# Stick-breaking attention: the queries' 1/rms inside the sigmoids, one scan for two heads, one split for two heads' result

## The chip, the core and the metric

The kernel runs on one core of a Trainium2 chip. That core has a tensor engine (PE, with its weight loads PEld), a vector engine (DVE), a scalar engine (ACT), a general engine (POOL), and a queue that issues loads (SP). Each of them works through its own list of instructions in order and waits on semaphores for the others. The metric is the device time of one execution in microseconds (us); lower is better.

## What is computed

A decoder trunk on 256 tokens of width 1024: one gMLP layer and one attention layer, each between two half-step SwiGLU FFNs, RMSNorm ahead of every part. The change is in the attention alone:

```python
def rms_norm(x, g):
    return x * lax.rsqrt(jnp.mean(x * x, axis=-1, keepdims=True) + NORM_EPS) * g

def one_block(qb, bi):                       # qb: (q * 1/sqrt(64)) of 128 queries, 16 heads
    mask = key_pos[None, :] < q_pos[:, None]
    z = jnp.einsum('bqkgd,bskd->bkgqs', qb, kf)
    log_1m_beta = jnp.where(mask, jax.nn.log_sigmoid(-z), 0.0)
    rev = lax.cumsum(log_1m_beta, axis=4, reverse=True)
    excl = jnp.concatenate([rev[..., 1:], jnp.zeros_like(rev[..., :1])], axis=-1)
    a = jnp.where(mask, jnp.exp(jax.nn.log_sigmoid(z) + excl), 0.0)
    return jnp.einsum('bkgqs,bskd->bqkgd', a, vf)

x = x + stick_breaking_attention(rms_norm(x, mix_norm) @ w_q, k, v) @ w_o
```

The kernel does this with products instead of sums of logarithms: a weight is sigmoid(z) times the product of sigmoid(-z) over the keys that lie between.

## The kernel before

**Products.** The residual stream lies transposed in SBUF (`xT`, features on partitions, tokens along the free axis). Every float32 operand is split into a high and a low part, and `mm3` (L145 to L150) makes each product of three matmuls: L148 high times low, L149 low times high, L150 high times high. `split` (L152 to L154) makes the parts: a cast on ACT, a subtraction on DVE. The weights stream in as 333 pieces of 128x1024, each loaded once and split by ACT (L81, `whi`) and DVE (L83, `wlo`) some pieces ahead of use. These splits run through the whole kernel, the attention too.

**1/rms.** `Rms.columns` (L305) makes 1/rms as two columns `rT`, one value per token on the partitions, and two diagonal blocks `diag` (L320). `Rms.rows` (L323) turns them into `rb`, the same values along the free axis on all partitions, with one product on PE (L324) and a copy on ACT (L325).

**Attention.** It goes by blocks of two heads, b = 0 to 7, in the order that `ATT_STEPS` writes down. For each block:
- q (`q_in`, `q_out`; one for four heads): 48 matmuls into a PSUM bank; L680 multiplies by 1/rms and 1/8 (`rb8`) on DVE into `qf`; then `qf` is split into `qh`, `ql`.
- z (`weights_of`): the scores of 128 queries at a time, so two banks per block: `z0` with 2x128 keys, `z1` with 2x256. ACT makes `keep` = sigmoid(-z) (L711) and `beta` = sigmoid(z) (L712). POOL masks both on the diagonal block (L718), and sets the last column of `keep` (L710).
- p (`products_of`): DVE runs the reversed product over `keep` with one scan per head and block of queries (L728), four per block of two heads; POOL (128 keys) or DVE (256 keys) multiplies it into `beta` (L729).
- t (`transposed`): six transposes on PE (L736 to L738) into two banks `at`, then splits into `a0h`, `a0l`, `a1h`, `a1l`.
- v (`values_of`): the products with v into a bank `o`; its two halves (one head each, on 64 partitions) are split into `oTh`, `oTl`, one after the other.
- o: 24 matmuls of `oT` with w_o into the four banks `yo`.

**What sets the order.** The program is traced in the order of `ATT_STEPS`, and a scheduler then orders each engine's list by priority and by its own model of durations, and puts in the waits. So an instruction that becomes shorter or goes away also moves others. Two limits matter here: the scores, transposes and results share four PSUM banks (pool `pg`), so a new z needs a bank that somebody has finished reading; and `beta`, `keep` and other short-lived tiles share eight SBUF buffers (pool `scr`).

Of the kernel before, what the change touches and what calls it, by code (L numbers as in the profile page):

```python
# [15 lines left out]
P = 128  # L16
T = 256
# [12 lines left out]
# The attention's order of issue, by blocks of two heads: q (four heads' queries), z (scores), p  # L30
# (weights), t (weights transposed), v (values), o (products into the residual stream, in the
# banks that y sets up).
# [6 lines left out]
class Weights:  # L39
    """The weight matrices as a stream of [128, 1024] pieces in the order of use. Each is loaded  # L40
    once and split exactly into two float32r parts, w = hi + lo, some pieces ahead of its use."""

    def __init__(self, tc, raw_pool, hi_pool, lo_pool):
# [3 lines left out]
        self.behind = 0  # so many pieces keep their place  # L47
# [12 lines left out]
    def order(self, ins):  # L60
        """Keeps an instruction behind those traced ahead of it, where the order matters."""
        return self.keep_order(ins) if self.strict else ins
# [37 lines left out]
def trunk(  # L100
# [44 lines left out]
    def mm3(o, a, b, first, last):  # L145
        """o (+)= a.T @ b for a, b each given as two float32r parts."""
# [9 lines left out]
    # The gMLP's blocks of 256 features: the u products, the mixing behind them, the products into  # L156
    # the residual stream behind that.
# [16 lines left out]
    def plan_in_out(n, ins, w_out):  # L174
        """Pairs of blocks: columns of the first matrix, then, one pair later, the rows that they
        meet in the second."""
# [66 lines left out]
    def warm_up(n):  # L243
        """Products of nothing, that wake the tensor engine's clock while the first loads run."""
        bank = gbank("warm")
        for _ in range(n):
            W.order(nc.tensor.matmul(bank[:, :P], ones, ones, start=True, stop=True))
# [17 lines left out]
    rb = act.tile([P, T], F32, name="rb")  # L265
    rT = act.tile([P, 2], F32, name="rT")
    diag = act.tile([P, 2, P], F32, name="diag")

    def prepare(d, gains, sq=True):
        """The parts of x*g of chunk d for the next products, and its share of the mean square."""  # L270
# [22 lines left out]
    def newton(o, root, v, w):  # L293
        """o = v**-0.5 from an estimate of v**0.5, with a step of Newton's; w is scratch."""
# [5 lines left out]
    class Rms:  # L300
        """1/rms of each token: first as a column per 128 tokens (rT), then along the free axis on
        all partitions (rb)."""
# [4 lines left out]
        def columns(self):  # L307
# [11 lines left out]
            for tt in range(2):  # L319
                nc.vector.tensor_scalar_mul(diag[:, tt, :], ident, rT[:, tt : tt + 1])  # L320
# [8 lines left out]
    def load_x(hf):  # L329
        """Half of x into the residual stream, its parts and its squares."""  # L330
# [33 lines left out]
    def bc2(ap):  # L364
        """[128, n] -> [128, 2, n], the same twice."""
# [6 lines left out]
    class Residual:  # L372
        """y.T = sum over chunks of W[chunk].T @ h[chunk], in four banks."""
# [13 lines left out]
    def close(y, tail, head, scale, gains):  # L387
        """The last chunks block by block, so that each block of x is ready early; head blocks of
        the first of them go ahead."""
# [11 lines left out]
    def project(outs, ids, xs, mid={}, by_bank=False):  # L401
        """outs += W.T x for blocks of 256 features: [features, tokens] of two halves each. mid:
        what else is done behind a number of groups."""
# [20 lines left out]
    def project_rows(o, ids, xs, mid={}):  # L424
        """x.T W for a block of 256 features: [tokens, features] of two halves."""
# [17 lines left out]
    def ffn_in(tag, j, ids, mid={}, by_bank=False):  # L443
        """silu(gate) * up of 256 features, in two parts."""
# [16 lines left out]
    def ffn(tag, plan, gains, mid={}, by_bank=False, extra={}):  # L461
        """extra: what else is done ahead of a block's products into the residual stream."""
# [439 lines left out]
```

## Time and profile before

| what | value |
|---|---|
| time, median of 3 runs | 1019.38 us (1019.08 to 1020.25) |
| span of the profiled execution, first to last instruction | 1016.9 us |
| PE busy in the span | 998.7 us (98%) |
| DVE, ACT, POOL busy | 651.4, 499.6, 84.0 us |
| the attention in the span, first q product to the last product with w_o | about 739 to 826 us |

The profile is of one execution, and its own total time isn't recorded beside the span; the median of the timed runs lies 2.4 us above the span, and what is saved inside the span is taken off the median. In the rows below, L numbers are lines of the kernel before. An idle time in brackets stands ahead of its instruction, with the instruction that ended the wait. A matmul's busy time overlaps the next one's: those of 256 columns are shown as 0.28 us and start 0.12 us apart.

### The profile page before, as it was taken

How to read it: one execution, taken by the hardware profiler on the slowest of the kernel's cores; microseconds unless marked ns; L12 is line 12 of the kernel's file. 1: busy time of each engine (PE TensorE's matmuls, PEld its weight loads, DVE VectorE, ACT ScalarE, POOL GpSimd, SP SyncE). 2: the span in 40 equal slices, each digit the busy share in tenths (PEclk: the TensorE clock that was granted, in tenths of full speed). 3: DMA queues.
4: the chain of work that ended last, by engine and by line, in shares of the span. 5: the costliest groups of instructions: out<-in, count | busy, mean ns of one | idle time of the engine just before them, and what ended most of it. 6: DMA issues, size and time to landing. Idle time of an engine off the chain costs nothing.

```text
span 1016.9 us, 19320 instructions
## 1 busy us (share of the span) xinstructions
PE 998.7 (98%) x8044; PEld 979.4 (96%) x8044; DVE 651.4 (64%) x852; ACT 499.6 (49%) x683; POOL 84.0 (8%) x122
## 2 busy tenths in 40 slices
PE   9999999999999999999999999999998899999997
PEld 8999999999999999999999999999998799999996
DVE  6865665676766774646569655564679975655553
ACT  7543434475544553434348444443476565444433
POOL 3000000010000300000003000000036420000002
PEclk9999999999999999999999999999999999999999
DMA  9965555656545365655564756555642436656511
GB/s 310 325 187 174 185 179 176 187 161 212 186 167 167 125 214 183 187 184 187 180 190 141 239 185 187 182 188 181 193 132 65 137 117 219 188 185 191 183 42 42
DMA packets 135208, 179.56 MB, mean 177 GB/s; under 512 B 5624, under 2 KB 119376, under 8 KB 135120
## 3 DMA queue, kind: packets, MB, share of 16 engines
q1 hardware_dynamic: 134768, 177.76, 54.9%
q8 instruction: 63, 1.03, 0.4%
q0 software_dynamic: 192, 0.52, 0.2%
q14 instruction: 25, 0.20, 0.1%
q10 hardware_dynamic: 160, 0.05, 0.0%
HBM read 176.73 MB, written 1.05 MB: 175 GB/s over the span
## 4 chain that ended last, share of the span: by engine, by line
PE 88%; DVE 6%; issue 2%; ACT 1%; DMA 1%; POOL 1%; SPq 0%; ACTq 0%; POOLq 0%; DVEq 0%
PE yo L148 2%; PE yo L150 2%; PE yo L149 2%; PE gb L148 2%; PE uc L149 2%; PE gc L148 2%; PE ub L149 2%; PE yb L148 2%; PE uc L150 2%; PE ub L150 2%; PE ub L148 2%; PE gb L150 2%; PE uc L148 2%; PE ud L150 2%; PE gc L150 2%
## 5 line engine op out<-in xcount | busy, mean ns | idle before, releaser
L81 ACT CAST whi<-raw 128x1024 fp32r<-128x1024 f32 (+1 forms) x333 | 342.3, 1044 | 403.3 <-issue 219.2
L83 DVE TENSOR_TENSOR wlo<-raw,whi 128x1024 fp32r<-128x1024 f32 (+1 forms) x333 | 400.9, 1221 | 203.2 <-ACT whi L81 202.4
L288 POOL TENSOR_TENSOR acc<-acc,sq 128x256 f32<-128x256 f32 x39 | 33.9, 870 | 566.9 <-ACT sq L287 564.9
L148 PE MATMUL ga<-xnh,wlo 128*128 128x256 f32 x176 | 50.7, 288 | 0.0
L148 PE MATMUL ya<-hha,wlo 128*128 128x256 f32 x176 | 50.0, 284 | 0.1
L148 PE MATMUL yc<-hhc,wlo 128*128 128x256 f32 x176 | 50.0, 284 | 0.1
L148 PE MATMUL yb<-hhb,wlo 128*128 128x256 f32 x176 | 50.0, 284 | 0.0
L148 PE MATMUL gd<-xnh,wlo 128*128 128x256 f32 x176 | 50.0, 284 | 0.0
L148 PE MATMUL gb<-xnh,wlo 128*128 128x256 f32 x176 | 49.9, 283 | 0.0
L148 PE MATMUL gc<-xnh,wlo 128*128 128x256 f32 x176 | 49.9, 283 | 0.0
L149 PE MATMUL ya<-hla,whi 128*128 128x256 f32 x176 | 49.8, 283 | 0.0
L149 PE MATMUL yb<-hlb,whi 128*128 128x256 f32 x176 | 49.8, 283 | 0.0
L149 PE MATMUL yc<-hlc,whi 128*128 128x256 f32 x176 | 49.7, 283 | 0.0
L150 PE MATMUL ud<-xnh,whi 128*128 128x256 f32 x176 | 49.7, 282 | 0.0
L150 PE MATMUL uc<-xnh,whi 128*128 128x256 f32 x176 | 49.6, 282 | 0.0
L149 PE MATMUL ub<-xnl,whi 128*128 128x256 f32 x176 | 49.6, 282 | 0.0
L149 PE MATMUL uc<-xnl,whi 128*128 128x256 f32 x176 | 49.6, 282 | 0.0
L150 PE MATMUL yb<-hhb,whi 128*128 128x256 f32 x176 | 49.6, 283 | 0.0
L148 PE MATMUL ua<-xnh,wlo 128*128 128x256 f32 x176 | 49.6, 282 | 0.0
L150 PE MATMUL ga<-xnh,whi 128*128 128x256 f32 x176 | 49.6, 282 | 0.0
L150 PE MATMUL ub<-xnh,whi 128*128 128x256 f32 x176 | 49.6, 282 | 0.0
L149 PE MATMUL gd<-xnl,whi 128*128 128x256 f32 x176 | 49.5, 281 | 0.0
(286 smaller groups left out, 3367.1 us busy)
## 6 DMA issues: line engine op xcount, KB each, us to landing
raw<-in_ffn_w_in_dram SPq DMA_DIRECT2D x176, 512.0 KB, 4.6
raw<-in_ffn_w_out_dram SPq DMA_DIRECT2D x88, 512.0 KB, 4.2
raw<-in_a_w_in_dram SPq DMA_DIRECT2D x32, 512.0 KB, 4.4
raw<-in_a_w_out_dram SPq DMA_DIRECT2D x16, 512.0 KB, 3.3
raw<-in_b_w_q_dram SPq DMA_DIRECT2D x8, 512.0 KB, 4.4
raw<-in_b_w_o_dram SPq DMA_DIRECT2D x8, 512.0 KB, 4.3
raw<-in_w_kv_dram SPq DMA_DIRECT2D x4, 512.0 KB, 4.2
xin<-in_x_dram SPq DMA_DIRECT2D x4, 256.0 KB, 4.5
```

The lines of the kernel that those rows point to most:

```text
L81: ins = nc.scalar.copy(hi[:, cc], raw[:, cc])
L83: ins = nc.vector.tensor_sub(lo[:, cc], raw[:, cc], hi[:, cc].bitcast(F32))
L148: nc.tensor.matmul(o, al, bh, start=first, stop=False, skip_group_check=True)
L149: nc.tensor.matmul(o, ah, bl, start=False, stop=False, skip_group_check=True)
L150: nc.tensor.matmul(o, ah, bh, start=False, stop=last, skip_group_check=True)
L288: nc.gpsimd.tensor_add(acc, acc, s)
```

## The change

Three edits in the attention, and one piece of memory that they need.

1. q isn't scaled any more: `q_out` splits the PSUM bank itself, without `qf`. The factor 1/rms/8 goes into the sigmoids as a scale per partition, since the scores have queries on partitions (`zscale`, two tiny tiles made from `rT`). So for this norm there is no `diag`, no product on PE and no `rb`.
2. One scan runs over both heads of a block of queries. `keep` of the two heads is one row of 2x(S+1) elements; the extra column of each head is 0 and not 1, and the scan's second operation adds a row that is 1 at the start of each head and 0 elsewhere, which restarts the product. That row is in `spare`, where `rb` and `diag` lie for the rest of the kernel; POOL fills it with four memsets.
3. The bank `o` is copied on ACT, 64 partitions at a time, into one tile `of`, and `of` is split by one cast and one subtraction over 128 partitions.

```diff
-    rb = act.tile([P, T], F32, name="rb")
     rT = act.tile([P, 2], F32, name="rT")
-    diag = act.tile([P, 2, P], F32, name="diag")
+    spare = act.tile([P, P + 1 + 2 * (T + 1)], F32, name="spare")
+    rb = spare[:, :T]
+    diag = spare[:, T : 2 * T].rearrange("p (n t) -> p n t", n=2)
...
             for tt in range(2):
-                nc.vector.tensor_scalar_mul(diag[:, tt, :], ident, rT[:, tt : tt + 1])
+                if self.tag != "m1":
+                    nc.vector.tensor_scalar_mul(diag[:, tt, :], ident, rT[:, tt : tt + 1])
...
     def q_out(j, bank):
-        qf = scratch(f"qf{j}")
-        nc.vector.tensor_mul(pair(qf), pair(bank), bc2(rb8))
...
-        split(qh, ql, qf)
+        split(qh, ql, bank)
...
-            nc.gpsimd.memset(keep[:, :, S : S + 1], 1.0)
-            nc.scalar.activation(keep[:, :, :S], z, AF.Sigmoid, scale=-1.0)
-            nc.scalar.activation(beta, z, AF.Sigmoid)
+            nc.gpsimd.memset(keep[:, :, S : S + 1], 0.0)
+            nc.scalar.activation(keep[:, :, :S], z, AF.Sigmoid, scale=zscale[1][:, tt : tt + 1])
+            nc.scalar.activation(beta, z, AF.Sigmoid, scale=zscale[0][:, tt : tt + 1])
...
-            for h in range(2):
-                rev = keep[:, h, :S][:, ::-1]
-                nc.vector.tensor_tensor_scan(rev, rev, rev, 1.0, ALU.mult, ALU.bypass)
+            rev = keep.rearrange("p h s -> p (h s)")[:, ::-1]
+            r0 = 0 if tt == 0 else P + 1
+            nc.vector.tensor_tensor_scan(
+                rev, rev, spare[:, r0 : r0 + 2 * (S + 1)], 0.0, ALU.mult, ALU.add
+            )
...
+        of = scratch(f"of{b}", T)
         for r in range(2):
             rr = slice(r * 64, (r + 1) * 64)
-            split(oT[0][rr, b, :], oT[1][rr, b, :], bank[rr, r * T : (r + 1) * T])
+            nc.scalar.copy(of[rr, :], bank[rr, r * T : (r + 1) * T])
+        split(oT[0][:, b, :], oT[1][:, b, :], of)
...
-    project([first[1]], [[i] for i in plan_q[1]], XN, {1: norm.rows})
-    nc.vector.tensor_scalar_mul(rb8, rb, 0.125)
+    project([first[1]], [[i] for i in plan_q[1]], XN)
+    for t, s in zip(zscale, (0.125, -0.125)):
+        nc.vector.tensor_scalar_mul(t, rT, s)
...
+    nc.gpsimd.memset(spare, 0.0)
+    for c in (0, P + 1, P + 1 + T + 1):
+        nc.gpsimd.memset(spare[:, c : c + 1], 1.0)
```

The lists of the engines change from the first q products on. On PE, around the transposes of block 0 (`at_0_...`), before; `q_9105` is q for heads 12 to 15, `z_0_8945` and `z_1_8954` are the scores of block 1:

```order
L150 MATMUL z_0_8945<-kzh,qh_8836 128x256
L148 MATMUL z_1_8954<-kzh,ql_8837 128x512
L149 MATMUL z_1_8954<-kzl,qh_8836 128x512
L150 MATMUL z_1_8954<-kzh,qh_8836 128x512
L148 MATMUL q_9105<-xnh,wlo_8731 128x256
L149 MATMUL q_9105<-xnl,whi_8730 128x256
L736 MATMUL at_0_8971<-ident,beta_0_8850 128x128
L150 MATMUL q_9105<-xnh,whi_8730 128x256
```

and after, the same place (`q_8873` is q for heads 8 to 11, `z_0_8980` the scores of block 2):

```order
L150 MATMUL q_8873<-xnh,whi_8700 128x256
L148 MATMUL z_0_8938<-kzh,ql_8832 128x256
L149 MATMUL z_0_8938<-kzl,qh_8831 128x256
L150 MATMUL z_0_8938<-kzh,qh_8831 128x256
L148 MATMUL z_1_8947<-kzh,ql_8832 128x512
L149 MATMUL z_1_8947<-kzl,qh_8831 128x512
L150 MATMUL z_1_8947<-kzh,qh_8831 128x512
L740 MATMUL at_0_8964<-ident,beta_0_8847 128x128
L741 MATMUL at_0_8964<-ident,beta_1_8856 128x128
L742 MATMUL at_0_8965<-ident,beta_1_8856 128x128
```

Before, the scores of block 0 stood behind 37 of the 48 products of the q for heads 8 to 11, and the first transpose of block 0 came 25 rows behind those scores, alone, with the other five after 14 more q products. After, the scores of block 0 stand ahead of all 48, the first transpose comes 60 rows behind them, and all six stand together. 24 products of the last q now stand together behind the transposes of block 2.

On DVE, the rows for block 6 before (`keep` is the scans):

```order
L728 SCALAR_TENSOR_TENSOR keep_0_9338<-keep_0_9338 128x128 x2
L728 SCALAR_TENSOR_TENSOR keep_1_9347<-keep_1_9347 128x256
L154 TENSOR_TENSOR oTl<-o_9359,oTh 64x256
L728 SCALAR_TENSOR_TENSOR keep_1_9347<-keep_1_9347 128x256
L154 TENSOR_TENSOR a0l_9385<-at_4_9376,a0h_9384 128x512
L154 TENSOR_TENSOR oTl<-o_9359,oTh 64x256
L729 TENSOR_TENSOR beta_1_9346<-beta_1_9346,keep_1_9347 128x512
L154 TENSOR_TENSOR a1l_9387<-at_4_9377,a1h_9386 128x256
L83 TENSOR_TENSOR wlo_9598<-raw_9475,whi_9597 128x1024
L83 TENSOR_TENSOR wlo_9639<-raw_9538,whi_9638 128x1024
```

and after:

```order
L730 SCALAR_TENSOR_TENSOR keep_0_9322<-keep_0_9322,spare 128x258
L730 SCALAR_TENSOR_TENSOR keep_1_9331<-keep_1_9331,spare 128x514
L733 TENSOR_TENSOR beta_1_9330<-beta_1_9330,keep_1_9331 128x512
L154 TENSOR_TENSOR a0l_9368<-at_4_9359,a0h_9367 128x512
L154 TENSOR_TENSOR oTl<-of_9350,oTh 128x256
L154 TENSOR_TENSOR a1l_9370<-at_4_9360,a1h_9369 128x256
L83 TENSOR_TENSOR wlo_9624<-raw_9521,whi_9623 128x1024
```

Four scans became two, two subtractions `oTl` one, and one weight split of this stretch moved elsewhere.

On ACT, from the scores of block 5 to the next weight split, before:

```order
L711 ACTIVATE keep_1_9258<-z_1_9253 128x2x256
L153 CAST oTh<-o_9270 64x256
L712 ACTIVATE beta_1_9257<-z_1_9253 128x512
L153 CAST a0h_9289<-at_3_9281 128x512
L153 CAST oTh<-o_9270 64x256
L153 CAST a1h_9291<-at_3_9282 128x256
L81 CAST whi_9597<-raw_9475 128x1024
```

and after:

```order
L712 ACTIVATE keep_1_9243<-z_1_9238,zscalen 128x2x256
L713 ACTIVATE beta_1_9242<-z_1_9238,zscalep 128x512
L763 COPY of_9262<-o_9255 64x256 x2
L153 CAST a0h_9275<-at_3_9267 128x512
L153 CAST oTh<-of_9262 128x256
L153 CAST a1h_9277<-at_3_9268 128x256
L81 CAST whi_9581<-raw_9459 128x1024
```

Both readings of `o` now stand together and on ACT alone, and the cast of the whole tile comes as a third instruction. With that the bank of `o` is free without DVE: in the lists of waits the scores `z_1` of blocks 3, 4, 6 and 7 waited for DVE before (a `pg` bank that `a0l` had to finish reading), and wait for PE and ACT after.

## Rows read from the trace of the kernel before

**Rows 1.** The page: busy time, share of the span and instructions of each engine.

```profile
PE 998.7 (98%) x8044; PEld 979.4 (96%) x8044; DVE 651.4 (64%) x852; ACT 499.6 (49%) x683; POOL 84.0 (8%) x122
```

**Rows 2.** Windows: stretch, its length, busy PE, PEld, DVE, ACT, POOL, PE clock, DMA.

```profile
739.43:760.00 20.57, 20.44 (x169) 20.05 (x168) 15.52 (x27) 16.05 (x26) 5.14 (x8) 1.00 0.38 125
760.00:805.00 45.00, 37.45 (x260) 33.25 (x259) 44.09 (x73) 29.61 (x62) 30.50 (x54) 1.00 0.34 107
805.00:826.00 21.00, 20.28 (x163) 19.48 (x162) 16.35 (x31) 14.00 (x30) 5.40 (x7) 1.00 0.30 99
```

**Rows 3.** Timeline of PE: start, length, instruction, [idle before, what ended it].

```profile
762.40 0.33 PE L736 MATMUL at<-ident,beta 128*128 128x128 f32 x1 [1.08 <-POOL beta L729]
765.27 0.33 PE L737 MATMUL at<-ident,beta 128*128 128x128 f32 x1 [0.89 <-DVE beta L729]
769.86 0.50 PE L149 MATMUL o<-a0l,vdh 128*128 128x512 f32 x1 [1.24 <-DVE a0l L154]
773.62 0.50 PE L148 MATMUL z<-kzh,ql 128*128 128x512 f32 x1 [0.47 <-DVE a0l L154]
789.98 0.50 PE L148 MATMUL z<-kzh,ql 128*128 128x512 f32 x1 [1.67 <-DVE a0l L154]
797.11 0.50 PE L148 MATMUL z<-kzh,ql 128*128 128x512 f32 x1 [1.24 <-DVE a0l L154]
803.68 0.50 PE L149 MATMUL o<-a0l,vdh 128*128 128x512 f32 x1 [0.70 <-DVE a0l L154]
816.25 0.74 PE L148 MATMUL yo<-oTh,wlo 128*128 128x256 f32 x4 [0.64 <-ACT oTh L153]
```

**Rows 4.** Timeline of PE at the product for `rb`.

```profile
750.93 0.60 PE L324 MATMUL pstm<-diag,ones 128*128 128x256 f32 x2
751.18 0.47 PE L148 MATMUL q<-xnh,wlo 128*128 128x256 f32 x1
751.49 0.28 PE L149 MATMUL q<-xnl,whi 128*128 128x256 f32 x1
```

**Rows 5.** Groups of DVE by form, 739 to 826: count, busy us, mean ns, idle before.

```profile
L728 DVE TENSOR_TENSOR_SCAN keep<-keep 128x256 f32<-128x256 f32 x16 | 11.9, 766 | 0.0
L728 DVE TENSOR_TENSOR_SCAN keep<-keep 128x128 f32<-128x128 f32 x16 | 7.9, 522 | 0.5 <-POOL keep L718 0.5
L154 DVE TENSOR_TENSOR oTl<-o,oTh 64x256 fp32r<-64x256 f32 x16 | 6.6, 414 | 0.7 <-ACT oTh L153 0.4
L680 DVE TENSOR_TENSOR qf<-q,rb 128x512 f32<-128x512 f32 x4 | 2.6, 676 | 0.0
L320 DVE TENSOR_SCALAR diag<-ident,rT 128x128 f32<-128x128 f32 x2 | 0.5, 284 | 0.0
```

**Rows 6.** Groups of ACT by form, 739 to 826.

```profile
L712 ACT ACTIVATE beta<-z 128x256 f32<-128x256 f32 x8 | 3.1, 391 | 0.0
L153 ACT CAST oTh<-o 64x256 fp32r<-64x256 f32 x16 | 5.8, 365 | 9.8 <-DVE oTl L154 7.3 <-PE o L150 2.2
L153 ACT CAST a1h<-at 128x256 fp32r<-128x256 f32 x8 | 3.0, 377 | 0.0
```

**Rows 7.** Tile `vsb` of the gMLP: activations with a scale per partition, min/median/max ns.

```profile
L552 ACT ACTIVATE vsb<-v,rT x16: 466/474/508, 216.0 to 250.8; 128x256 f32<-128x256 f32 x16
```

**Rows 8.** Timeline of ACT: the load of the sigmoid's table and the first sigmoid.

```profile
758.12 1.28 ACT L711 ACT_TABLE_LOAD   x1 [0.84 <-PE z L150]
759.41 0.39 ACT L711 ACTIVATE keep<-z 128x256 f32<-128x256 f32 x1
```

**Rows 9.** Timeline of DVE: the subtraction `a0l` of two successive blocks.

```profile
789.27 0.66 DVE L154 TENSOR_TENSOR a0l<-at,a0h 128x512 fp32r<-128x512 f32 x1
796.39 0.66 DVE L154 TENSOR_TENSOR a0l<-at,a0h 128x512 fp32r<-128x512 f32 x1
```

**Rows 10.** Timeline of POOL: the multiplication at block 0 and at a later block.

```profile
761.71 0.64 POOL L729 TENSOR_TENSOR beta<-beta,keep 128x256 f32<-128x256 f32 x1 [0.38 <-DVE keep L728]
788.00 1.78 POOL L729 TENSOR_TENSOR beta<-beta,keep 128x256 f32<-128x256 f32 x1 [0.70 <-DVE keep L728]
```

More of the change, by code (lines that the diff above doesn't have):

```diff
@@ L674, in trunk @@
     ffn("c", plan10, [(("mix", 1), xnh, xnl)])
-    rb8 = act.tile([P, T], F32, name="rb8")
+    zscale = [at.tile([P, 2], F32, name=f"zscale{n}") for n in "pn"]
     oT = [at.tile([P, KC, T], F32R, tag=f"big{p}", name=f"oT{p}") for p in "hl"]
     def q_out(j, bank):
-        qf = scratch(f"qf{j}")
-        nc.vector.tensor_mul(pair(qf), pair(bank), bc2(rb8))
         qh = hp.tile([P, 512], F32R, tag="hh", name=f"qh{j}")
         ql = hp.tile([P, 512], F32R, tag="hl", name=f"ql{j}")
-        split(qh, ql, qf)
+        split(qh, ql, bank)
         return qh, ql
```

## The prediction

> **What bounds the kernel now.** I read the page's busy line first. PE is busy for 998.7 of 1016.9 us [rows 1], so only what PE waits for in some stretch, or what it does itself, can be taken off. Then the windows: in the attention PE sits idle for 20.57 - 20.44 = 0.13, 45.00 - 37.45 = 7.55 and 21.00 - 20.28 = 0.72 us, together 8.4 us, and nearly all of that lies between 760 and 805, where DVE is busy for 44.09 of 45 us [rows 2]. So in this stretch DVE sets the pace. PE's timeline names the waits: eight stalls, 7.93 us in all, six of which end on a DVE row, one on a POOL row that multiplies what DVE has just scanned, the last on ACT [rows 3]. A stall costs PE a little more than its bracket: matmuls of 256 columns start 0.12 us apart but are shown 0.28 us long [rows 4], so 0.16 us more is lost at each stop. The prize is thus 8.4 + 8 x 0.16 = 9.7 us, and PE's own work besides.
>
> **The change, part by part.** The profiled span is 1016.9 us. I take the terms off it, and the same off the median of 1019.38.
>
> *1/rms into the sigmoids.* PE loses one product: q products stand at 750.93 + 0.56 = 751.49 where without it the second would stand at about 751.05, so 0.44 us comes off PE's own list [rows 4]. That is gained in full, since PE is busy there. DVE loses four `qf` of 0.676 us and two `diag` of 0.284 [rows 5], 3.3 us, and gains two operations on 2 columns, for which the 0.284 of `diag` is an upper end: net -2.7 us. ACT gains a scale per partition in 32 sigmoids. The nearest rows are gelus with such a scale, 474 ns, against sigmoids of the same shape without one, 391 [rows 6, 7]: 83 ns, 2.7 us in all (lower end nothing, if it is the function that costs more). The Trainium skill, "ScalarE: Activation LUTs", section "What ACT_TABLE_LOAD costs", speaks against this edit more strongly: each pointer operand adds about 93 ns, which would be 3.0 us. The sum would be the same by either, as long as ACT has room: 29.61 of 45 us busy [rows 2].
> A wait is added: the sigmoids wait for `zscale`, which is two weight splits behind `rT` on DVE, and behind the sigmoids ACT holds the next weight casts. Against that, z no longer waits for `rb` at all. In the new PE list the scores of block 0 stand 37 products earlier, 37 x 0.12 = 4.4 us. The table load, which waited 0.84 us for z [rows 8], and the first sigmoid come some 4 us earlier, limited by ACT's casts ahead of them.
>
> *One scan for two heads.* Before, 16 scans of 128 at 522 ns and 16 of 256 at 766 [rows 5]: 1.91 ns per element and 278 ns per scan. After, 8 of 258 and 8 of 514: 278 + 258 x 1.91 = 771 and 1260 ns. So 20.6 us become 16.2, less what successive instructions overlap (0.08 us of each of 16): 3.1 to 4.4 us saved. I take 3.1. The add in the second operation has no row. It is the same instruction with two inputs, so I take the same rate; the ends are 0 and twice the rate (a rival below).
>
> *One split for two heads' result.* DVE: 16 `oTl` of 0.414 us become 8 of the same length along the free axis: 2.7 to 3.3 us less [rows 5]. ACT: 16 casts of 0.365 become 16 copies of the same shape, and 8 casts of 128x256 come on top, by the nearest row 0.377 each [rows 6]: +3.0 us. But ACT's second cast now waits for DVE's subtraction of the first half (7.3 us of ACT idle [rows 6]); with `o` read by ACT alone this wait goes, and so does PE's wait for a free bank that ends on `a0l`.
>
> *Memsets.* POOL's four stand ahead of the sums of squares, when POOL has nothing to do, and wait only for the last FFN's use of `rb`. I cost them at nothing; the cover is an engine busy for 84 us of the span [rows 1].
>
> DVE loses 2.7 + 3.1 + 2.7 = 8.5 us. What that is worth follows from one block: `a0l` recurs after 7.12 us [rows 9]. Over the same block PE's start recurs after 797.11 - 789.98 = 7.13 us, with the stall of 1.24 + 0.16 [rows 3] and a short one of 0.3 in it: PE itself needs 5.4. After, DVE's block is shorter by two scans' fixed parts (0.4), one subtraction (0.34) and one weight split that the new list moves out of this stretch (1.2): 5.2 us. So PE leads again, but barely, and stalls will be left.
>
> Stall by stall [rows 3]:
> - 762.40 and 765.27 (1.08, 0.89: transposes of block 0). Between its scores and its transposes lie now 48 q products and a block's scores, 5.8 + 1.1 us, and the chain starts 4 us earlier. Both go: 1.97.
> - 769.86 (1.24, first result on `a0l`). DVE's list still has two masked scans, a multiplication and weight splits ahead of that `a0l`. I leave 1.0: gain 0.24.
> - 773.62 (0.47, z of block 3). The bank is now freed by ACT, but PE arrives at the next result earlier than DVE does: I put 0.8 there, a loss of 0.33.
> - 789.98 and 797.11 (1.67, 1.24: z of blocks 6 and 7 on `a0l`). Freed by ACT's copies: 2.91.
> - 803.68 (0.70) and 816.25 (0.64): DVE is about level with PE at the first, and at the second the chain is two copies and a cast, then the subtraction. Half of each: 0.67.
>
> Sum 5.46, plus 0.16 for each of the four that vanish, 0.64, plus 0.44 on PE: 6.5 us. Span 1010.4, **time 1012.9 us**.
>
> **The rivals.**
> - *All stalls vanish.* Speaks for it: PE's 5.4 against DVE's 5.2 per block. Against: the first two results stand right behind DVE's fullest stretch. Gain 9.7 + 0.44: 1009.2.
> - *DVE still leads.* If the weight split isn't spared in the end (it must run somewhere), DVE's block is 7.12 - 0.74 = 6.4 us, 1.0 more than PE's, over six blocks 6.0 of the 9.7: gain 3.7 + 0.44, 1015.2.
> - *POOL is shut out by longer scans.* A multiplication on POOL takes 0.64 us alone and 1.78 beneath two scans [rows 10]: POOL stands still while DVE scans. A single scan of 1.26 us holds it for 0.5 longer than one of 0.77, and the mask that the next scan waits for may come just then: 8 x 0.5 = 4.0 of the 6.5 lost, 1016.9. Against it: the scans' total is less than before. The Trainium skill, "GPSIMD Engine Reference", section "Key points", has POOL share its SBUF interfaces with DVE and contend with instructions of two SBUF inputs; by that rule the eight new `oTl`, which read SBUF twice and no PSUM, hold POOL as well. The trace agrees for the scans; no row here shows it for `oTl`.
> - *ACT takes the lead.* It gains 4 x 83 + 377 = 0.71 us per block, and PE's z now waits on ACT's copies. If ACT's list were the path in five of the eight blocks, 3.5 us: 1016.4. Against it: 15.4 us of room in 45 [rows 2].
> - *Slower: the scan with an add is slow.* 8 x 772 = 6176 elements pass through the scans; at twice the rate, +11.8 us of DVE against the 8.5 saved, on an engine that is 98% busy: +3.3 - 0.44, 1022.2. It decides from 1.91 + 8.5 / 6176 = 3.3 ns per element. Against it: 1.91 ns is what a serial product costs already, and the old scan ran the same instruction.
> - *No change.* Each saved wait is followed by another of the same length on ACT or POOL: about 1018.9 with PE's 0.44.
>
> **How the numbers follow.** Forecast 0.48, all stalls gone 0.13, DVE still leads 0.17, POOL 0.06, ACT 0.05, no change 0.06, slower 0.05. A gain above 0.2% (2.0 us, about what can be told from no change) comes from the first five: 0.89, less 0.01 for the low edges of the last two, 0.88. Same 0.07, slower 0.05. The range goes from 1009.2, where no stall is left, to 1016.9, the POOL case; what lies outside is no change, slower and the edges of three cases, under 0.2.
>
> **What would show it.** Right: no product for `rb` at this norm; first sigmoid 3 to 5 us earlier against the q products; no PE wait for z that ends on `a0l`; PE idle between the first q product and the close down from 8.4 to 2 to 4 us, the rest on `o` behind `a0l`; scans near 770 and 1260 ns; ACT without waits for `oTl`. Wrong: scans above 3.3 ns per element; POOL rows of over 1.3 us in the path; ACT at over 90% in the attention with PE's z behind its copies; DVE still above 95%.

## The result, and the profile after

| | us | against before |
|---|---|---|
| before, median of 4 runs | 1019.44 (1019.08 to 1020.25) | |
| after, median of 4 runs | 1003.86 (1002.06 to 1004.66) | 0.9841, 95% interval 0.9829 to 0.9853 |
| predicted | 1012.9 (1009.2 to 1016.9) | |

Faster, as forecast, but by 15.6 us and not by 6.5. That is more than the 10.1 us that the prediction held to be all that could be won. So something was gained where the prediction did not look. The first line of the page of after answers to [rows 1] (busy time, share, instructions):

```profile
PE 982.3 (98%) x8042; PEld 963.5 (96%) x8042; DVE 645.2 (64%) x823; ACT 504.1 (50%) x690; POOL 86.5 (9%) x126
```

PE has two matmuls fewer, and yet 16.4 us less busy time. The span fell by 14.2 us, from 1016.9 to 1002.7, and the median by 15.6. The difference is the two profiled executions: in the runs of both kernels whose span is recorded, the time lies 1.7 to 1.8 us above the span, so before's profile is of an execution of about 1018.6, quicker than its median, and after's is of 1004.40, slower than its median. Three marks on PE tell where the span fell:

| stretch | before | after | difference |
|---|---|---|---|
| start of the span to the first q product | 739.43 | 727.22 | -12.21 |
| first q product to the last FFN's first product | 80.65 | 79.13 | -1.52 |
| from there to the end | 196.86 | 196.33 | -0.53 |

The change touches the middle stretch alone, and that gave 1.5 us. The instructions ahead of the first q product are the same in both kernels, in the same order on every engine, but for POOL's four memsets (0.9 us at 717.5). What differs there is how fast PE runs the same products. Durations (shortest, median, longest, in ns) of one kind of product of the third FFN, before:

```profile
L148 PE MATMUL uc<-xnh,wlo x176: 277/279/285, 552.8 to 728.4; 128*128 128x256 f32 x176
```

and after:

```profile
L148 PE MATMUL uc<-xnh,wlo x176: 276/276/276, 545.7 to 716.2; 128*128 128x256 f32 x176
```

The starts tell it better, since durations overlap. Four neighbours in after's timeline (start, busy us):

```profile
611.30 0.28 PE L148 MATMUL gc<-xnh,wlo 128*128 128x256 f32 x1
611.42 0.28 PE L149 MATMUL gc<-xnl,whi 128*128 128x256 f32 x1
611.53 0.28 PE L150 MATMUL gc<-xnh,whi 128*128 128x256 f32 x1
611.64 0.28 PE L148 MATMUL gc<-xnh,wlo 128*128 128x256 f32 x1
```

They start 0.34 us apart over three products, 113 ns each. In before six products of the same kind take 0.71 us, 118 ns each:

```profile
623.32 0.28 PE L148 MATMUL gc<-xnh,wlo 128*128 128x256 f32 x1
...
624.03 0.28 PE L148 MATMUL uc<-xnh,wlo 128*128 128x256 f32 x1
```

Over all gate and u products of the four FFNs the mean distance of two starts is 118.3 ns before and 115.1 after. With the gMLP's u and the q products these are 4800; 4800 x 3.2 ns = 15.4 us, an estimate, where the first and the last stretch of the table show 12.7.

In the attention the windows of after answer to [rows 2] (us, then busy time of PE, PEld, DVE, ACT, POOL, granted clock, DMA share, GB/s):

```profile
727.22:747.80 20.58, 20.44 (x170) 20.03 (x169) 16.25 (x27) 17.32 (x28) 9.20 (x14) 1.00 0.46 147
747.80:792.80 45.00, 36.40 (x264) 32.88 (x263) 38.25 (x49) 32.14 (x66) 27.51 (x47) 1.00 0.31 98
792.80:806.35 13.55, 13.46 (x107) 12.84 (x106) 8.51 (x17) 8.73 (x20) 0.09 (x1) 1.00 0.37 117
```

PE's idle time is 0.14 + 8.60 + 0.09 = 8.8 us, where it was 8.4. DVE, which had been busy for 44.09 of 45 us, is down to 38.25, so it was relieved as planned, and PE waits as long as ever. Four stops now take the place of the eight of [rows 3]:

```profile
755.38 0.49 PE L149 MATMUL o<-a0l,vdh 128*128 128x512 f32 x1 [3.52 <-DVE a0l L154]
...
761.23 0.50 PE L149 MATMUL o<-a0l,vdh 128*128 128x512 f32 x1 [1.45 <-DVE a0l L154]
...
778.61 0.50 PE L148 MATMUL o<-a0h,vdl 128*128 128x512 f32 x1 [2.40 <-DVE a0l L154]
...
790.75 0.50 PE L149 MATMUL o<-a0l,vdh 128*128 128x512 f32 x1 [1.16 <-DVE a0l L154]
```

So there are two questions: what made the same products faster outside the attention, and why the attention gave so little.

### The profile page after: what moved, and what is told of

Its sections match the earlier page's. It is cut to its first block, busy times and chain, and to the rows that moved or that the text cites. A ratio compares the mean times of both kernels' runs of the same rounds, so it can differ in the third digit from the quotient of the medians.

```text
span 1002.7 us, 19306 instructions
## 1 busy us (share of the span) xinstructions
PE 982.3 (98%) x8042; PEld 963.5 (96%) x8042; DVE 645.2 (64%) x823; ACT 504.1 (50%) x690; POOL 86.5 (9%) x126
## 4 chain that ended last, share of the span: by engine, by line
PE 89%; DVE 5%; ACT 2%; issue 1%; DMA 1%; POOL 1%; SPq 0%; ACTq 0%; POOLq 0%; DVEq 0%
PE yo L148 2%; PE yo L150 2%; PE yo L149 2%; PE yb L148 2%; PE yb L150 2%; PE yb L149 2%; PE ud L148 2%; PE ud L150 2%; PE gd L148 2%; PE ud L149 2%; PE gb L148 2%; PE gd L150 2%; PE gd L149 2%; PE ub L148 2%; PE gc L150 2%; PE gb L150 2%
## 5 line engine op out<-in xcount | busy, mean ns | idle before, releaser
L149 PE MATMUL ga<-xnl,whi 128*128 128x256 f32 x176 | 49.3, 280 | 0.5 <-DVE xnl L277 0.5
L150 PE MATMUL ya<-hha,whi 128*128 128x256 f32 x176 | 49.4, 283 | 0.0
L150 PE MATMUL gd<-xnh,whi 128*128 128x256 f32 x176 | 49.4, 281 | 0.0
L148 PE MATMUL ud<-xnh,wlo 128*128 128x256 f32 x176 | 49.4, 281 | 0.0
L149 PE MATMUL ud<-xnl,whi 128*128 128x256 f32 x176 | 49.4, 281 | 0.0
L150 PE MATMUL yc<-hhc,whi 128*128 128x256 f32 x176 | 49.4, 283 | 0.0
```

The costliest lines, as they stand in the source:

```text
L148: nc.tensor.matmul(o, al, bh, start=first, stop=False, skip_group_check=True)
L149: nc.tensor.matmul(o, ah, bl, start=False, stop=False, skip_group_check=True)
L150: nc.tensor.matmul(o, ah, bh, start=False, stop=last, skip_group_check=True)
```

## Experiments on the products' pace: where the tiles lie

The diff holds a clue that I had passed over. `rb8` (1024 bytes per partition) goes, `rb` and `diag` (2048) become `spare` (2572, which takes up 2592), and so every tile that is allocated behind them moves 480 bytes down in SBUF: the weight pieces, the parts of h, scratch, k and v. The parts of the residual stream, `xnh` and `xnl`, lie ahead of them and stay. For a gate or u product, `xnh` or `xnl` is the moving operand and a weight piece the stationary one. All buffers of one kind repeat at multiples of 256 bytes, so one number tells how a pair lies: the start of the weight pieces minus the start of the stream, modulo 256. I call it the distance. Before it is 32 (76352 - 27168), after 64.

**e1**: the kernel before, with the tiles where the changed kernel has them.

```diff
-    rb8 = act.tile([P, T], F32, name="rb8")
+    gap = act.tile([P, 136], F32, name="gap")    # nobody uses it
...
-    nc.vector.tensor_scalar_mul(rb8, rb, 0.125)  # and bc2(rb8) in q_out
+    nc.vector.tensor_scalar_mul(rb, rb, 0.125)   # and bc2(rb) in q_out
```

> The kernel before, with every tile behind the residual stream (weight pieces, parts of h, scratch, k, v) 480 bytes further down in SBUF, where the changed kernel has them: rb is scaled in place, rb8 goes, and a gap that nobody uses fills up. The instructions are the same. Theory 'place': 12.2 of the 14.2 us were gained ahead of the first q product, in stretches whose instructions the change leaves alone, and what differs there is the place of the tiles; so this kernel gets them: 1019.4 - 12.7 = about 1006.7, with products of the third FFN about 115.5 ns apart, where they were 118.8. Rival 'edits': the gain comes from the three edits in some other way (what they leave behind on DVE or in the queues), and this kernel stays at 1019.4.

Measured: 1004.59 us (1003.67 to 1004.94), 0.9854 (0.9839 to 0.9869). With none of the three edits, the time is within 0.8 us of the changed kernel's.

**e2**: the changed kernel, with the tiles where the kernel before has them.

```diff
+    zscale = [act.tile([P, 2], F32, name=f"zscale{n}") for n in "pn"]   # from the pool att
+    gap = act.tile([P, 104], F32, name="gap")
```

> The changed kernel with all its tiles at the places that the kernel before has (an unused gap behind spare). Theory 'place': the 12.7 us outside the attention are lost again, 1003.9 + 12.7 = about 1016.6, and what is left against the kernel before, 2 to 3 us, is what the three edits are worth. Rival 'edits': 1003.9 stays.

Measured: 1018.94 us (1017.70 to 1019.64), 0.9992 (0.9983 to 1.0002). By the medians the three edits together are worth 0.7 us, and the interval includes nothing at all. From the first q product to the last FFN's first, e2 takes 79.2 us, as after does, where before takes 80.6: inside the attention the edits gain 1.4 us. The "2 to 3 us" that I still expected of them is not there.

**e3** and **e4** shift by 32 and by 512 bytes (`gap` of 248 and of 128 columns).

> As the first kernel, but shifted by 32 bytes and not 480. The weight pieces then start at 32 over a multiple of 64 bytes, as they do in the changed kernel. If what counts is this remainder, about 1006.7; if it is the distance of 480 bytes itself, or some coarser grid, this kernel stays near 1019.4 or lands between.

> As the first kernel, but shifted by 512 bytes: the remainder to 64 is again that of the kernel before. If the remainder counts, 1019.4; if any shift of this size does it (480 or 512 alike), about 1006.7.

Measured: 1028.36 us for 32 (1.0090, 1.0074 to 1.0107) and 1019.74 for 512 (1.0001, 0.9992 to 1.0011). The shift by 32 fits no theory that I had named: it is slower than before by 8.7 us. Its distance is 0, and its products start 120.0 ns apart. In all kernels up to here the products into the residual stream (y) take 119.6 to 120.0 ns, and there the parts of h and the weight pieces also have a distance of 0. That led to the theory that the distance decides.

**e6** and **e13** move the stream and leave the weight pieces: e6 in the kernel before (an unused gap of 96 bytes ahead of `xT`), e13 in e1 (64 bytes).

```diff
+    gap = act.tile([P, 24], F32, name="gap")     # e13: 16
     xT = act.tile([P, KC, T], F32, name="xT")
...
     diag = act.tile([P, 2, P], F32, name="diag")
+    gap2 = act.tile([P, 232], F32, name="gap2")  # e13: 120; what lies behind stays
```

> The kernel before with its weight pieces and everything behind them where they were, and the residual stream with its parts xnh and xnl moved up by 96 bytes, which makes the distance of xnh and the weight pieces 64 modulo 128. Theory 'distance': about 1004.6, as the kernel shifted by 480. Rival 'weights' (or any other tile behind the residual stream): 1019.5.

> The kernel before with the weight pieces where the changed kernel has them, and the residual stream moved up by 64 bytes, so that the distance modulo 128 is 0. Theory 'distance': the gate and u products fall back to 120.0 ns, and the time goes from 1004.6 to about 1028, as in the kernel shifted by 32. Rival 'weights': their place is unchanged, so 1004.6 stays.

Measured: 1015.09 us for e6, a third of the gain, and 1028.61 for e13. e13 decides it. Its weight pieces lie as in e1, the stream 64 bytes further up, the distance is 0, and it is 24.0 us slower than e1 with the same instructions. The same rows as above, for e13:

```profile
L148 PE MATMUL uc<-xnh,wlo x176: 283/283/283, 559.4 to 736.9; 128*128 128x256 f32 x176
```

```profile
625.02 0.28 PE L149 MATMUL gc<-xnl,whi 128*128 128x256 f32 x1
625.14 0.28 PE L150 MATMUL gc<-xnh,whi 128*128 128x256 f32 x1
625.26 0.28 PE L148 MATMUL gc<-xnh,wlo 128*128 128x256 f32 x1
625.38 0.28 PE L149 MATMUL gc<-xnl,whi 128*128 128x256 f32 x1
```

**e7, e14, e15, e16, e17** fill in other distances in the same way (e7 in the changed kernel, the others in the kernel before; e14 and e15 move both operands).

> The changed kernel with everything behind the residual stream 32 bytes further up: a distance of 96 modulo 128, the one that hasn't been run. Theory 'distance', taken as symmetric about 64: like 32, about 1018.9. If the time falls further with the distance: 1003 or less.

> The kernel before with a distance of 64 modulo 128, both operands moved by 64 against the first kernel: the stream at 96, the weight pieces at 32 modulo 128, so both are 32 over a multiple of 64. If the distance and the place modulo 64 are all that counts: about 1004.6, with about two thirds of the gate and u stretches at 113 ns and one third at 118. If the place modulo 128 counts as well: like the kernel with the stream moved by 96, about 1015.

> As e14, but with both operands on a multiple of 64 bytes (stream at 64, weight pieces at 0 modulo 128), the distance again 64. If the place modulo 64 decides between 113 and 118 ns: like the kernel with the stream moved by 96, about 1015, nearly all stretches at 118. If not: about 1004.6.

> The kernel before with everything behind the residual stream 160 bytes further down: the weight pieces lie 128 behind the stream modulo 256. If the period is 128 bytes, this is a distance of 0: products 120 ns apart, about 1028. If it is 256: something else, and from the neighbours (96: 1018.5 in the changed kernel, 192: 1015 to 1017) between 1004 and 1019.

> As e16, with a distance of 160 modulo 256. If the period is 128 bytes: as the kernel before (32), 1019.6, with spacings that jitter between 115 and 124 ns. If it is 256: not bound to that, 1004 to 1019.

Measured, with the mean distance of two starts over all gate and u products of the four FFNs (some 4160 pairs in each profile):

| distance modulo 256 | kernels | ns per gate or u product | time, us |
|---|---|---|---|
| 0 | e3, e13 | 119.96, 119.96 | 1028.36, 1028.61 |
| 32 | before, e2, e4 | 118.32, 118.31, 118.31 | 1019.44, 1018.94, 1019.74 |
| 64 | after, e1, e15 | 115.09, 115.04, 115.00 | 1003.86, 1004.59, 1004.60 |
| 96 | e7 | 117.94 | 1018.45 |
| 128 | e16 | 119.01 | 1022.79 |
| 160 | e17 | 119.97 | 1027.82 |
| 192 | e6, e14 | 117.57, 117.58 | 1015.09, 1016.81 |

One mean pace for each distance, whichever operand was moved, and never the same for 64 and 192 or for 0 and 128. So the period is not 128 bytes, as I had supposed from e5 to e15; 256 fits all that was run. 224 was not run for these products.

The same traces hold a test that no run was made for. In the gMLP's v products the roles are swapped: the weight piece moves and the stream is stationary. So their distance, stationary minus moving, is the table's with the sign turned: 224 where the gate and u products have 32. Their mean distances of two starts (378 pairs in each profile, stops left out) follow the table within 0.4 ns, but for 64, where they are in one of two paces: 119.97 and 119.96 ns at 0 (e3, e13), 114.45 and 117.77 at 64 (e6, e14), 117.54 at 96 (e17), 118.64 at 128 (e16), 119.97 at 160 (e7), 117.2 to 117.7 at 192 (after, e1, e15), and 116.7 at 224 (before, e2, e4).

**e5** and **e18** try the rule on another pair, the y products, with a gap of 64 and of 192 bytes ahead of the parts of h: their distance becomes 192 and 64. e5 is the changed kernel, e18 the fastest kernel so far (e9, below).

```diff
+    gap = ctx.enter_context(tc.tile_pool(name="gap", bufs=1)).tile([P, 16], F32, name="gap")   # e18: 48
     hp = ctx.enter_context(tc.tile_pool(name="hp", bufs=4))
```

> The changed kernel with an unused gap of 64 bytes ahead of the pool hp, so that the parts of h (the moving operand of the products into the residual stream, y) no longer have the same remainder to 128 bytes as the weight pieces (the stationary one), but differ by 64. Theory 'distance': what sets a product's time is where its moving operand lies against the next stationary one, modulo 128 bytes. The u and gate products took 120.0 ns apart at a distance of 0 (the kernel shifted by 32), 118.8 at 32 (before) and 113 to 118 at 64 (the changed kernel); the y products have had a distance of 0 in all of them, and 119.7 ns. With 64 they fall to 114 to 118 ns: 1968 products in three FFNs and the gMLP by 2 to 6 ns are 4 to 11 us, so 993 to 1000. Rival 'weights': it is the remainder of the weight pieces alone; then the y products stay at 119.7 and the time at 1003.9.

> The fastest kernel so far (pins, and the multiplication on DVE: 998.6) with an unused gap of 192 bytes ahead of the pool hp: the weight pieces then lie 64 behind the parts of h modulo 256, as they do behind the stream. If the rule of the distance holds for the y products too: they fall from 119.6 to 113 or 118 ns, as the gate and u products do (about 115.3 on average over their stretches), 1968 products by 4.3 ns = 8.5 us, so about 990; the last FFN's products of 512 columns, where h is the stationary operand, may cost up to 2.6 us of it, as at 192. If y has a rule of its own: 998.6, or 996 with 118 ns throughout.

Measured: in e5 y takes 117.8 ns, as other products do at 192, but the time is 1005.57 us: the last FFN's products of 512 columns, where h is the stationary operand, went from 227.1 to 233.1 ns, and the third FFN's gate and u products, whose operands had not moved, from 113.5 to 117.7; the last FFN's, not moved either, went from 117.6 to 115.8. In e18 y takes 115.7 ns, and one kind of product of the third FFN shows 276 as its median duration, where the changed kernel has 283:

```profile
L149 PE MATMUL yc<-hhc,wlo x176: 276/276/384, 568.6 to 727.9; 128*128 128x256 f32 x176
```

e18 takes 995.32 us (994.86 to 1001.61), 0.9777 (0.9745 to 0.9809): 3.3 us less than e9, not the 8.5 that I expected; one of its four runs took 1001.61, the others at most 995.45. The gate and u products, whose operands had not moved, shifted again: those of the first FFN from 115.0 to 117.0 ns and of the second from 114.1 to 117.8, those of the last from 117.6 to 114.2.

These shifts between two paces stay open. At a distance of 64 whole blocks of an FFN run at 113 to 114 ns and others at 117 to 118. The changed kernel's last FFN is in the slower one from end to end (start 0.70 us apart over six products):

```profile
890.73 0.28 PE L148 MATMUL ud<-xnh,wlo 128*128 128x256 f32 x1
...
891.43 0.28 PE L148 MATMUL gd<-xnh,wlo 128*128 128x256 f32 x1
```

What puts a block into one or the other isn't settled; e5 says that it is not the block's own addresses alone. Nor do the runs show the mechanism behind the distance. They show that the pace of gate and u, v and y products goes with where the two operands that PE itself reads start against each other. That the two reads hold each other up is the nearest explanation, and it is not shown.

## Experiments on the attention: where 6.5 us went

Here stretches are compared, from the first q product to the last FFN's first: 80.65 us before, 79.13 after. In three of the profiles compared here (e1, e10, e12) the granted clock fell to the 1.2 GHz level for 3.4 or 6.8 us in the attention. Their stretches (80.7, 79.9, 80.4 us) hold that as well, so for them the waits and the medians are read.

**Each edit by itself.** e12 is e1 with the first edit alone; e10 and e11 are the changed kernel with the second and the third undone. All lie at a distance of 64.

```diff
# e12: of the change, only q_out without qf, zscale, the sigmoids' scale, and no diag and rb at this norm
# e10: the changed kernel, with
+            for h in range(2):
+                rev = keep[:, h, :S][:, ::-1]
+                nc.vector.tensor_tensor_scan(rev, rev, rev, 1.0, ALU.mult, ALU.bypass)
# e11: the changed kernel, with
+            split(oT[0][rr, b, :], oT[1][rr, b, :], bank[rr, r * T : (r + 1) * T])
```

> The kernel before at the changed kernel's places, with the first of the three edits alone: 1/rms in the sigmoids, no qf, no product for rb. By the prediction 0.44 us of PE and the two waits at block 0's transposes (1.97): the stretch 80.7 becomes 78 to 78.5. If the earlier scores only shift these waits to the next block: 80 to 80.5.

> The changed kernel with the scans as they were, one per head (and no row of restarts), all else and all places as in the changed kernel. Read by the stretch from the first q product to the first product of the last FFN: 79.1 us in the changed kernel, 80.7 in the kernel before at the same places. If the scan over two heads gave its share of DVE's time (3.8 us less by the profile), the stretch is 80 to 82 us here; if its longer hold on POOL costs as much, 79; if it costs more, 77 to 78.

> The changed kernel with two heads' result split in two halves, as before. By the prediction's list this part took the waits of z for a0l away (2.9 us) and 2.7 us off DVE, so the stretch would be 81 to 82 us where it is 79.1; if those waits only moved to the result's own a0l, 79.

Measured: e12 1004.34 us (1003.16 to 1005.23) against e1's 1004.59: no gain. PE's waits in the attention are 7.0 us in both. The two waits at block 0's transposes are gone, and this one is there instead:

```profile
754.90 0.80 PE L148 MATMUL o<-a0h,vdl 128*128 128x512 f32 x1 [3.47 <-DVE a0l L154]
```

e10 1004.03 us (1002.50 to 1004.41) against after's 1003.86: the longer scan is worth nothing that can be measured. PE's waits in the attention are 6.7 us with the old scans, 8.5 with the new, and POOL's multiplication takes 828 ns on average with the old, 1137 with the new. e11 1005.47 us (1005.02 to 1007.65), and a stretch of 81.3 us: the split of two heads' result in one is worth 1.6 us by the medians and 2.2 by the stretch. Its waits (us in all, times, longest) hold what the prediction's list said would go:

```profile
PE z L148 <- DVE oTl L154: 3.5, 2, 3.3
```

**Why `a0l` is late.** DVE's timeline in after, up to the first stop:

```profile
750.61 0.68 DVE L730 TENSOR_TENSOR_SCAN keep<-keep,spare 128x258 f32<-128x258 f32 x1
752.48 1.44 DVE L730 TENSOR_TENSOR_SCAN keep<-keep,spare 128x514 f32<-128x514 f32 x1 [1.19 <-POOL keep L711]
754.03 0.69 DVE L733 TENSOR_TENSOR beta<-beta,keep 128x512 f32<-128x512 f32 x1
754.64 0.68 DVE L154 TENSOR_TENSOR a0l<-at,a0h 128x512 fp32r<-128x512 f32 x1
```

and POOL's beside it:

```profile
748.97 1.39 POOL L719 TENSOR_SCALAR_AFFINE_SELECT beta<-beta 128x256 f32<-128x256 f32 x1
751.44 0.64 POOL L733 TENSOR_TENSOR beta<-beta,keep 128x256 f32<-128x256 f32 x1 [1.08 <-DVE keep L730]
752.04 0.41 POOL L719 TENSOR_SCALAR_AFFINE_SELECT keep<-keep 128x256 f32<-128x256 f32 x1
752.39 0.10 POOL L711 MEMSET keep<- 128x2 f32 x1
```

The parts of block 0 that `a0l` needs were there at 750.1 (ACT's `a0h` runs from 749.54). DVE's list, however, has both scans of block 1 ahead of it. The second of them waits for a mask on POOL, the mask stands in POOL's list behind a multiplication, and that waits for the first scan. (The profile names the memset of L711 for this wait, but that ends at 752.49, behind the scan's start at 752.48; the mask ends at 752.45.) So two engines hand the work to and fro while PE stands still. Before, PE stopped at the transposes of block 0 instead, ahead of this place [rows 3].

**e8** puts this order right by pins alone: POOL's multiplication behind the block's masks, the scans behind `a0l` and `a1l` of the block before, the steps t ahead of p. **e9** takes POOL's multiplication to DVE besides.

```diff
-    "z0 p0 q2 z1 t0 z2 p1 v0 p2 t1 z3 v1 t2 q3 p3 z4 p4 y o0 z5 v2 "
-    "t3 o1 p5 z6 v3 p6 t4 o2 z7 v4 t5 o3 p7 v5 t6 o4 v6 t7 o5 v7 o6 o7"
+    "z0 p0 q2 z1 t0 z2 p1 v0 t1 p2 z3 v1 t2 q3 p3 z4 t3 p4 y o0 z5 v2 "
+    "t4 o1 p5 z6 v3 t5 p6 o2 z7 v4 t6 p7 o3 v5 o4 v6 t7 o5 v7 o6 o7"
...
+            if b - 1 in last:
+                behind(ins, last[b - 1])         # each scan, behind a1l of block b - 1
-            (nc.vector if tt else nc.gpsimd).tensor_mul(beta, beta, keep[:, :, 1 : S + 1])
+            ins = (nc.vector if tt else nc.gpsimd).tensor_mul(beta, beta, keep[:, :, 1 : S + 1])
+            if not tt:
+                behind(ins, mask[b])             # e8; in e9 nc.vector multiplies both
```

> The changed kernel with its order in the attention mended by pins alone: on POOL the multiplication of a block stands behind both of that block's masks, on DVE the scans of a block stand behind a0l and a1l of the block before, and the steps t come ahead of p. The work is the same. Theory 'order': the 8.5 us that PE still waits for a0l in the changed kernel (3.5 at the first result) come from a0l standing behind two scans that wait for POOL; they shrink to 2 to 3 us, and the time to about 998. Rival 'work': DVE simply has that much to do there, and waits come back elsewhere: 1003 to 1005.

> As the kernel with pins, but DVE now multiplies the block of 128 keys too, where POOL did (the pin on POOL goes). In the kernel with pins PE waits 6.3 us for its transposes, 5.6 of them on POOL, whose multiplication stands behind the masks and runs beneath a scan. Theory 'POOL': without POOL's multiplication these waits shrink to 2 to 3 us, at the price of 8 x 0.41 us on DVE, which has 6 us of room in 45; the stretch from the first q product to the last FFN's first falls from 78.1 to about 75, the time to about 999. Rival 'chain': the wait is for the chain scan, scan, multiply, whoever multiplies: 1002 to 1004.

Measured: e8 1002.46 us (1001.43 to 1003.23), 1.4 less than the changed kernel, about a quarter of what theory 'order' had, and a stretch of 78.1 us. No wait on `a0l` is left, but PE now waits for its transposes:

```profile
PE at L753 <- POOL keep L720: 3.4, 3, 1.7
PE at L753 <- POOL beta L744: 2.2, 2, 1.4
...
PE at L754 <- DVE beta L744: 0.7, 2, 0.5
```

e9 998.57 us (998.37 to 999.94), 0.9795 (0.9779 to 0.9812), a stretch of 74.3 us. Its waits in the attention, and its middle window:

```profile
PE at L751 <- DVE beta L744: 2.6, 4, 1.1
...
PE at L752 <- DVE beta L744: 0.4, 1, 0.4
```

```profile
746.70:791.70 45.00, 41.85 (x302) 38.12 (x301) 42.66 (x60) 35.17 (x72) 20.52 (x40) 1.00 0.34 104
```

DVE is busier than in after (42.66 against 38.25): it has POOL's multiplications besides, and in this window it no longer waits for POOL. PE is busier too (41.85 against 36.40). e9 is 5.3 us below the changed kernel and 6.0 below e1, which lies at the same distance. This is about the gain that the prediction had given to the three edits, but it comes with the order and the multiplication changed as well. No run has these two without the three edits, so how much of the 6.0 us needs the edits stays open.

## Why the prediction was wrong, step by step

**What bounds the kernel now.** Here the prediction failed first and by most. "The prize is thus 8.4 + 8 x 0.16 = 9.7 us, and PE's own work besides" takes the pace of PE's products as given wherever the change adds or removes none. The change moved the weight pieces against the stream, and the mean pace of the gate and u products went from 118.3 to 115.1 ns. By e1 that is 15.1 us (1019.67, the kernel before on the same chip, less 1004.59), nearly the whole result. No term, no bound and no rival of the prediction has it.

**1/rms in the sigmoids.** The terms were right, but by e12 the edit alone gains nothing, since one wait of 3.47 us came for the two that went (1.97 us together). The product for `rb` is gone, and the first sigmoid comes 742.38 - 727.22 = 15.2 us behind the first q product, where it came after 20.0 [rows 8]. ACT's price was right too (forecast 83 ns for each scale):

```profile
L712 ACT ACTIVATE keep<-z,zscalen 128x256 f32<-128x256 f32 x8 | 3.9, 484 | 0.0
L713 ACT ACTIVATE beta<-z,zscalep 128x256 f32<-128x256 f32 x8 | 3.9, 481 | 0.2 <-POOL keep L711 0.2
```

That is 90 ns above the 391 of [rows 6]. The 93 ns that the Trainium skill gives ("ScalarE: Activation LUTs", "What ACT_TABLE_LOAD costs") is nearer than my 83.

**One scan.** 771 and 1260 ns were forecast; the means are 758 and 1342. Beyond the fixed 278 ns that is at most 2.1 ns per element, where the rival of the slow scan begins at 3.3, and DVE was relieved of 20.6 - 16.8 = 3.8 us (forecast 3.1 to 4.4):

```profile
L730 DVE TENSOR_TENSOR_SCAN keep<-keep,spare 128x514 f32<-128x514 f32 x8 | 10.7, 1342 | 2.9 <-POOL keep L711 2.4 <-POOL keep L719 0.5
L730 DVE TENSOR_TENSOR_SCAN keep<-keep,spare 128x258 f32<-128x258 f32 x8 | 6.1, 758 | 0.3 <-POOL keep L719 0.3
```

**One split.** DVE's part went from 6.6 to 3.5 us, ACT no longer waits for `oTl`, and no z waits for `a0l`: right in kind, and e11 puts it at 1.6 to 2.2 us, where the list had 2.9.

**Stall by stall.** This is the step that failed inside the attention. The stops that were to go did go. What was to come in their place was mis-sized: at the first result 1.0 us was left and 3.52 came, at the next 0.8 and 1.45 came, and 2.40 at 778.61, where a z had waited before, and 1.16 at 790.75. The list left about 2.5 us of 7.9; 8.5 were measured. I had read from the lists that the transposes come later, and drew the gain from that, but I did not follow `a0l` through DVE's and POOL's lists, where both scans and the multiplication stand ahead of it.

**The block of 7.12 us.** DVE's 5.2 us against PE's 5.4 counted DVE's work and not its waits. In after DVE has 45.00 - 38.25 = 6.8 us of idle time in the window where it had 0.9, nearly all behind POOL. `a0l` recurs after 5.92 and 6.21 us there (777.88, 783.80, 790.01), not after 5.2. The 5.4 us of PE were misread too: between 789.98 and 797.11 the trace of before has no other wait than the one of 1.24, so the 0.3 that was taken off isn't there, and PE needs 5.7.

**The rivals.** "POOL is shut out" had the right mechanism: the multiplication that took 0.64 us alone takes 1.40 beneath a scan of 514, and it stands in the chain that PE waits for, a sign that the prediction had named:

```profile
775.43 1.40 POOL L733 TENSOR_TENSOR beta<-beta,keep 128x256 f32<-128x256 f32 x1 [0.69 <-DVE keep L730]
```

The rival was given 0.06 and a price of 4.0 us. By e10 the length of the scans is worth 1.8 us of PE's waits and nothing in the time; what the order and POOL's multiplication cost together is 5.3 us (after against e9). With the tiles where they were (e2), the time of 1018.94 is that of the rival "no change" (1018.9), which had 0.06 as well. So the right sign of the forecast owes little to its reasons: of the 15.6 us, 0.7 by the medians or 1.4 by the stretch came from the edits, the rest from where the tiles happened to land.

## What to carry to other kernels

When a change adds, drops or resizes a tile, ask which tiles move, and compare the mean distance of two starts of products that the change doesn't touch; a gain there may belong to the layout, and an unused gap can test it, as it gives or takes such a gain (here 24 us between two layouts of the same instructions). Test an edit with all other tiles held in place before believing what it gained. And a relieved engine is worth only what its list lets through: follow the one instruction that PE waits for through the lists of all engines that feed it, and put that order right first.

## What the runs showed of the hardware that I had not expected

- The time of a 128x256 product depends on where its two SBUF operands start relative to each other: 115.0 to 120.0 ns on average over the gate and u products by the distance modulo 256, the same for each distance in up to three layouts, and nearly the same for the v products with the roles swapped. The Trainium skill, "SBUF — State Buffer", section "Who interferes with whom", gives PE two independent read ports, one for the moving operand and one for the weight load, and has PE never wait for anyone. By that rule e1 and e13 would take the same time; they differ by 24.0 us, so here the measurement decides.
- At a distance of 64 a product has two paces, 113 to 114 and 117 to 118 ns, that hold through whole blocks; it is open what chooses.
- POOL's instructions take longer beneath DVE instructions that read two SBUF operands, the new `oTl` among them: a mask of 0.41 us took 0.69 when it began beside `oTl` (778.47 and 778.48 in after), and 0.68 to 0.69 at the same place in e2, e5, e7 and e10. The prediction had the rule from the Trainium skill ("GPSIMD Engine Reference", "Key points") and no row for `oTl`; these rows agree.
